# A decoder trunk's feed-forward stages: sums of weight quarters by adding transfers and on VectorE instead of GpSimd

## The chip, the cores and the metric

The kernel runs on one core of a Trainium2 chip. The metric is the device time of one execution in microseconds, as the median of several runs. TensorE does the matrix products (its 128x128 weight loads are shown apart from the matmuls); VectorE, ScalarE (ACT) and GpSimd (POOL) work beside it; SyncE (SP) issues the transfers from HBM. Each engine works off its own queue of instructions in order, and waits at an instruction until the semaphores that it names have been reached.

## The reference

A trunk of two layers on x of 512 tokens by 1024, all in float32. Each layer is a half-step feed-forward, a mixer (layer 0: gated linear recurrence and mLSTM heads; layer 1: sparse attention), and a second half-step feed-forward; then a last RMSNorm. The change touches the four feed-forwards alone:

```python
def rmsnorm(x, g):
    xf = x.astype(jnp.float32)
    y = xf * lax.rsqrt(jnp.mean(xf * xf, axis=-1, keepdims=True) + EPS)
    return (y * g.astype(jnp.float32)).astype(x.dtype)

def swiglu_ffn(x, w_gu, w_down):        # D_MODEL = 1024, D_FF = 2816
    gate, up = jnp.split(x @ w_gu, 2, axis=-1)
    return (jax.nn.silu(gate) * up) @ w_down
```

A layer adds half of `swiglu_ffn(rmsnorm(x, g), ...)` to x.

## The kernel before

Everything lies with the features on the 128 partitions and the 512 tokens along the free axis. A float32 operand is held as two fp32r halves: `hi`, a copy by ACT, and `lo`, the rest, by one subtraction. A product is three matmuls (hi hi, hi lo, lo hi; `mm3`, L172 to L176). Stages run in the order f0a (first feed-forward of layer 0), ab (mixer), f0b, f1a, nsa (mixer), f1b.

A feed-forward (`ffn`, L369 on) has 22 blocks of 128 hidden units. The first four (`CLASSIC`) are done plainly, gate and up each with weights of 128x1024 loaded and split by `wload` (L162 to L170; for the blocks 2 and 3 GpSimd makes `lo`). Meanwhile `Quarters` (L238 to L276) makes sums of quarters of the normalized x (K halves by token halves), splits each (ACT L255, VectorE L256), and two of the sums are GpSimd's (L263, L270). The other 18 blocks are "pairs": gate and up of a block as one 2x2 product by seven multiplications instead of eight (Winograd's form), each of 12 matmuls of 128x256, so 84 for a pair.

`Pair.load` (L291 to L317) brings a pair's weights as four quarters of 128x512: three loads on SP (512, 256 and 256 KB), four sums by GpSimd (L301 to L304), and four splits, each an ACT copy (L310) and a VectorE subtraction (L311), three of 128x1024 and one of 128x512. The raw quarters and sums lie in two buffers `ra` and `rc` (named r in the trace); there are two such sets, taken in turn, so that the loads of a pair wait until the splits of the pair two before have read theirs. The split halves lie in five buffers, taken in turn: three pairs `whi`, `wlo`, and two `wx`.

The products `p1` to `p7` (L323 to L363) come in the order p1, p7, p3 of the pair before, p6, p2, p4, p5; the last pair of a stretch ends p5, p4, p3. They share accumulators: bank `a` takes the first, sixth, fifth and third products one after another, `e` the seventh and fourth, and a bank of its own the second. After each the sum so far is read out: by ACT (L327, L340, L345, L360) or added by VectorE (L333, L350, L355). L362 multiplies the two halves into the hidden block, and ACT L380 and VectorE L381 split that.

After 8, 16 and 22 hidden blocks the down projection adds what is there into X (L444 to L451): eight tiles of `wd`, each loaded, split (L168, L169) and multiplied. So each feed-forward has three stretches of pairs, of 4, 8 and 6, with a down projection (D) behind each. The code orders TensorE's instructions by hand (`manual_schedule`); the other engines' order comes from a scheduler by priorities (`SAHEAD` for a pair's load and splits, `EV` for what empties a bank), so it is seen in the built program alone. In stage ends GpSimd also adds the squares for the next norm (L115), whose root (L141), row sums and broadcast R (L142 to L149) the next stage needs.

## Time and profile before

| | us |
|---|---|
| median of 3 runs (2118.14 to 2119.45) | 2118.43 |
| the profiled execution | 2126.54 |
| its span, first to last instruction | 2124.8 |
| TensorE busy | 2019.0 (95%) |
| VectorE busy | 1432.3 (67%) |
| ACT busy | 1015.2 (48%) |
| GpSimd busy | 858.3 (40%) |
| mean granted clock of TensorE | 0.974 of full |

The shares are means over all stages: where TensorE is idle, and for whom it waits there, is read from the waits and from the windows of the single stretches.

### The profile page before, as it was taken

To read this page: it belongs to the slowest core of one execution; us is meant where nothing else is said; L and a number is where in the kernel's file an instruction comes from. 1 tells how busy PE (TensorE), PEld (TensorE's weight loads), DVE (VectorE), ACT (ScalarE), POOL (GpSimd) and SP (SyncE) were. 2 spreads that over 40 slices of the span, in tenths; PEclk is the share of its full clock that TensorE was granted. 3 is DMA by queue.
4 is the path that set the end of the run, shared out by engine and by line. 5 is a ranking of instruction groups with operands and counts; after the bars stand their busy time and mean duration, and the time that the engine had idled before them with its cause. 6 is when DMAs were issued, how large, how long until landed. Compare 5 with 4: busy or idle time off the path is not lost.

```text
span 2124.8 us, 30587 instructions
## 1 busy us (share of the span) xinstructions
PE 2019.0 (95%) x11896; PEld 1753.4 (83%) x11896; DVE 1432.3 (67%) x2021; ACT 1015.2 (48%) x1828; POOL 858.3 (40%) x602
## 2 busy tenths in 40 slices
PE   7999999989998999999999999999999989999997
PEld 5889889767787889898798989877777667889896
DVE  4957757488658759485866947443877778659474
ACT  4535436445544435254543525434877754435252
POOL 6425523243134427163433614202655554427152
PEclk8999999999899999999999999999999999999998
DMA  4233322222132323233232333321100032323212
GB/s 160 80 110 95 115 75 75 90 80 90 60 99 80 108 81 112 83 101 94 80 110 90 100 94 95 119 84 60 36 16 30 17 114 70 100 90 108 86 61 84
DMA packets 73585, 182.09 MB, mean 86 GB/s; under 512 B 7264, under 2 KB 8032, under 8 KB 73440
## 3 DMA queue, kind: packets, MB, share of 16 engines
q1 hardware_dynamic: 73296, 180.06, 26.7%
q8 instruction: 93, 1.52, 0.3%
q14 instruction: 52, 0.43, 0.1%
q10 hardware_dynamic: 144, 0.09, 0.0%
HBM read 178.02 MB, written 2.10 MB: 85 GB/s over the span
## 4 chain that ended last, share of the span: by engine, by line
PE 75%; DVE 12%; issue 4%; ACT 3%; POOL 3%; DMA 1%; SPq 0%; POOLq 0%; DVEq 0%; ACTq 0%
PE ps L174 18%; PE ps L175 18%; PE ps L176 18%; PE pt L175 3%; PE pt L176 3%; PE pt L174 3%; PE px L977 2%; PE pt L772 2%; DVE wx L311 1%; DVE wlo L169 1%; DMA r<-wgu 1%; PE pt L993 1%; DVE h L381 1%; DVE t L362 1%; DVE wlo L311 1%
## 5 line engine op out<-in xcount | busy, mean ns | idle before, releaser
L301 POOL TENSOR_TENSOR r<-r,r 128x512 f32<-128x512 f32 x72 | 124.0, 1723 | 627.7 <-DMA r<-wgu 587.8
L168 ACT ACTIVATE whi<-raw 128x1024 fp32r<-128x1024 f32 (+2 forms) x196 | 193.2, 987 | 368.9 <-PE ps L175 268.2
L175 PE MATMUL ps<-h,whi 128*128 128x512 f32 x704 | 277.2, 394 | 0.5 <-DVE h L381 0.5
L174 PE MATMUL ps<-h,whi 128*128 128x512 f32 x704 | 276.3, 393 | 0.9 <-ACT h L380 0.9
L176 PE MATMUL ps<-h,wlo 128*128 128x512 f32 x704 | 276.5, 393 | 0.0
L311 DVE TENSOR_TENSOR wlo<-r,whi 128x1024 fp32r<-128x1024 f32 (+1 forms) x174 | 237.2, 1365 | 50.3 <-ACT whi L310 48.9
L310 ACT ACTIVATE whi<-r 128x1024 fp32r<-128x1024 f32 (+1 forms) x174 | 165.5, 951 | 188.5 <-PE ps L175 129.4
L169 DVE TENSOR_TENSOR wlo<-raw,whi 128x1024 fp32r<-128x1024 f32 (+2 forms) x150 | 186.7, 1246 | 76.4 <-ACT whi L168 71.6
L450 DVE SCALAR_TENSOR_TENSOR X<-ps,X 128x512 f32<-128x512 f32 x96 | 66.4, 691 | 253.9 <-PE ps L176 253.9
L169 POOL TENSOR_TENSOR wlo<-raw,whi 128x1024 fp32r<-128x1024 f32 (+1 forms) x46 | 108.7, 2364 | 257.0 <-ACT whi L168 247.5
L311 DVE TENSOR_TENSOR wx<-r,wx 128x1024 fp32r<-128x1024 f32 (+1 forms) x114 | 170.2, 1493 | 57.5 <-ACT wx L310 57.1
L174 PE MATMUL ps<-x,whi 128*128 128x512 f32 x432 | 179.7, 416 | 0.4 <-ACT x L103 0.4
L174 PE MATMUL ps<-qB,whi 128*128 128x256 f32 x520 | 148.5, 286 | 25.0 <-DVE t L355 25.0
L176 PE MATMUL ps<-x,wlo 128*128 128x512 f32 x432 | 171.5, 397 | 0.0
L175 PE MATMUL ps<-x,whi 128*128 128x512 f32 x432 | 171.0, 396 | 0.3 <-DVE x L104 0.3
L175 PEld LDWEIGHTS ps<-h,whi 128*128 128x128 f32 x704 | 132.9, 189 | 31.0 <-DVE h L381 2.3
L174 PEld LDWEIGHTS ps<-h,whi 128*128 128x128 f32 x704 | 133.0, 189 | 30.7 <-ACT h L380 1.8
L176 PEld LDWEIGHTS ps<-h,wlo 128*128 128x128 f32 x704 | 132.8, 189 | 28.6
L115 POOL TENSOR_TENSOR acc<-acc,t 128x512 f32<-128x512 f32 x48 | 74.8, 1558 | 189.4 <-ACT t L113 178.3
L175 PE MATMUL ps<-qB,whi 128*128 128x256 f32 x520 | 146.4, 282 | 0.0
L176 PE MATMUL ps<-qB,wlo 128*128 128x256 f32 x520 | 146.4, 282 | 0.0
L303 POOL TENSOR_TENSOR r<-r,r 128x512 f32<-128x512 f32 x72 | 134.3, 1865 | 5.3
(341 smaller groups left out, 5897.7 us busy)
## 6 DMA issues: line engine op xcount, KB each, us to landing
r<-wgu SPq DMA_DIRECT2D x72, 512.0 KB, 3.9
r<-wgu SPq DMA_DIRECT2D x144, 256.0 KB, 2.8
raw<-wd SPq DMA_DIRECT2D x64, 512.0 KB, 3.5
raw<-wgu SPq DMA_DIRECT2D x30, 512.0 KB, 3.6
raw<-wd SPq DMA_DIRECT2D x32, 384.0 KB, 3.1
raw<-ab_fm SPq DMA_DIRECT2D x21, 512.0 KB, 3.5
raw<-nsa_fm SPq DMA_DIRECT2D x17, 512.0 KB, 3.5
raw<-ab_out SPq DMA_DIRECT2D x8, 512.0 KB, 3.6
```

Source lines behind the costliest of these rows:

```text
L115: nc.gpsimd.tensor_add(acc, acc, sq)
L168: nc.scalar.activation(hi[:, :n], raw[:, :n], AF.Copy)
L169: (eng or nc.vector).tensor_sub(lo[:, :n], raw[:, :n], hi[:, :n].bitcast(F32))
L174: nc.tensor.matmul(ps, wh, xh, start=start, stop=False, skip_group_check=on)
L175: nc.tensor.matmul(ps, wh, xl, start=False, stop=False, skip_group_check=on)
L176: nc.tensor.matmul(ps, wl, xh, start=False, stop=stop, skip_group_check=on)
L301: nc.gpsimd.tensor_sub(ra[:, 1], rc[:, 3], ra[:, 0])
L303: nc.gpsimd.tensor_sub(ra[:, 2], rc[:, 1], ra[:, 0])
L310: nc.scalar.activation(hi[:, :m], src, AF.Copy)
L311: nc.vector.tensor_sub(lo[:, :m], src, hi[:, :m].bitcast(F32))
L450: nc.vector.scalar_tensor_tensor(X[i], ps, 0.5, X[i], op0=OP.mult, op1=OP.add)
L772: nc.tensor.matmul(p2[m][:, :155].rearrange("p (g n) -> p g n", g=5), w[:, q * 256 + m * P:q * 256 + (m + 1) * P], tt[:, :, n:n + 8 * 30 + ...
```

## The change

In each pair, the four GpSimd sums go. The quarters are now loaded so that two of the four positions of `ra` hold the one quarter and two the other (a source with a repeated part), and a third transfer, issued by GpSimd, adds another quarter to the two middle positions while it lands (`accum_op`). Two sums remain and are VectorE's (L309, L310). The sums differ in sign from before, so that the quarters of x whose names begin with B are negated. In the classic part, VectorE makes the low halves and quarter sums that were GpSimd's. The first product is copied by ACT from bank `a` to a second bank `b`, on which the second product then accumulates, so that VectorE's add L333 goes. The fifth product is copied out by ACT to a buffer `u4`, from which VectorE adds (L362). Lines behind L261 are 1 to 8 further down.

```diff
@@ -252,26 +252,31 @@
             def split(self, name, src):
                 t = blk(self.qb[QS.index(name)], F32R, f"q{name}")
                 hi, lo = (t[:, n * 4 * H:(n + 1) * 4 * H].rearrange("p (k t) -> p k t", k=4) for n in range(2))
-                nc.scalar.activation(hi, src, AF.Copy)
-                nc.vector.tensor_sub(lo, src, hi.bitcast(F32))
+                if name[0] == "B":
+                    nc.scalar.activation(hi, src, AF.Copy, scale=-1.0)
+                    nc.vector.scalar_tensor_tensor(lo, src, -1.0, hi.bitcast(F32), op0=OP.mult, op1=OP.subtract)
+                else:
+                    nc.scalar.activation(hi, src, AF.Copy)
+                    nc.vector.tensor_sub(lo, src, hi.bitcast(F32))
                 self.Q[name] = hi, lo
             def before(self):
                 b11, b12, b21, b22 = self.f
                 nc.vector.tensor_sub(b22, b12, b22)
                 self.split("B11", b11)
-                nc.gpsimd.tensor_sub(b12, b12, b11)
+                nc.vector.tensor_sub(b12, b12, b11)
                 self.split("Q7", b22)
                 nc.vector.tensor_sub(b11, b11, b22)
                 self.split("Q6", b11)
             def after(self):
                 q6, q5, b21, b22 = self.f
-                nc.gpsimd.tensor_add(b22, q5, q6)
                 self.split("B21", b21)
                 nc.vector.tensor_sub(b21, b21, q6)
                 self.split("Q4", b21)
                 self.split("Q5", q5)
+                nc.vector.tensor_add(b22, q5, q6)
                 self.split("B22", b22)
         turns = [0, 0]
@@ -295,15 +300,16 @@
                     ra, rc = (blk(rb[2 * (turns[1] % 2) + i], F32, f"r{i}")[:, :4 * T]
                               .rearrange("p (s c) -> p s c", s=4) for i in range(2))
                     turns[1] += 1
-                    nc.sync.dma_start(ra[:, 0:4:3], w[0].rearrange("p (s c) -> p s c", s=2))
-                    nc.sync.dma_start(rc[:, 3], w[1][:, :T])
-                    nc.sync.dma_start(rc[:, 0], w[1][:, T:])
-                    nc.gpsimd.tensor_sub(ra[:, 1], rc[:, 3], ra[:, 0])
-                    nc.gpsimd.tensor_add(rc[:, 1], rc[:, 0], rc[:, 3])
-                    nc.gpsimd.tensor_sub(ra[:, 2], rc[:, 1], ra[:, 0])
-                    nc.gpsimd.tensor_sub(rc[:, 2], ra[:, 3], ra[:, 2])
-                    for src, names in ((ra[:, 0:2], ("B11", "Q7")), (ra[:, 2:4], ("Q6", "B21")),
-                                       (rc[:, 0:2], ("Q4", "Q5")), (rc[:, 2:3], ("B22",))):
+                    both = lambda src: src.unsqueeze(1).to_broadcast([P, 2, T])
+                    nc.sync.dma_start(ra[:, 0:2], both(w[0][:, :T]))
+                    nc.sync.dma_start(ra[:, 2:4], both(w[1][:, T:]))
+                    nc.sync.dma_start(rc[:, 0], w[0][:, T:])
+                    nc.gpsimd.dma_start(ra[:, 1:3], both(w[1][:, :T]), accum_op=OP.add)
+                    nc.vector.tensor_add(rc[:, 1], ra[:, 0], ra[:, 2])
+                    nc.vector.tensor_add(rc[:, 2], rc[:, 0], rc[:, 1])
+                    for src, names in ((ra[:, 0:2], ("B11", "Q7")), (rc[:, 0:2], ("B21", "Q6")),
+                                       (ra[:, 2:4], ("Q5", "Q4")), (rc[:, 2:3], ("B22",))):
                         hi, lo = parts()
                         m = len(names) * T
                         src = src.rearrange("p s c -> p (s c)")
@@ -321,17 +327,16 @@
                     mm3(ps[:, :H], wh[:, ks], wl[:, ks], xh[:, k], xl[:, k], start and k == 0, k == 3, not start)
             def p1(self):
-                self.a, self.t1 = psum(), tp.tile([P, T], F32, name="t1", bufs=3)
+                self.a, self.b, self.t1 = psum(), psum(), tp.tile([P, T], F32, name="t1", bufs=3)
                 self.product(self.a, "B11", True)
                 with tc.high_priority(offset=EV):
-                    nc.scalar.activation(self.t1[:, :H], self.a[:, :H], AF.Copy)
+                    nc.scalar.activation(self.b[:, :H], self.a[:, :H], AF.Copy)
             def p2(self):
-                b = psum()
-                self.product(b, "B21", True)
+                self.product(self.b, "B21", False)
                 with tc.high_priority(offset=EV):
-                    nc.vector.tensor_add(self.t1[:, :H], b[:, :H], self.t1[:, :H])
-                nc.scalar.activation(self.t1[:, :H], self.t1[:, :H], AF.Silu)
+                    nc.scalar.activation(self.t1[:, :H], self.b[:, :H], AF.Silu, scale=-1.0)
             def p7(self):
                 self.e, self.t2 = psum2(), tp.tile([P, T], F32, name="t2", bufs=3)
@@ -351,13 +356,15 @@
             def p5(self):
                 self.product(self.a, "Q5", False)
+                u4 = tp.tile([P, H], F32, name="u4", bufs=1)
                 with tc.high_priority(offset=EV):
-                    nc.vector.tensor_add(self.t2[:, H:], self.a[:, :H], self.t2[:, H:])
+                    nc.scalar.activation(u4, self.a[:, :H], AF.Copy)
+                    nc.vector.tensor_add(self.t2[:, H:], u4, self.t2[:, H:])
             def p3(self):
                 self.product(self.a, "B22", False)
                 with tc.high_priority(offset=EV):
-                    nc.scalar.activation(self.t1[:, H:], self.a[:, :H], AF.Silu)
+                    nc.scalar.activation(self.t1[:, H:], self.a[:, :H], AF.Silu, scale=-1.0)
                 with tc.high_priority(offset=EV // 2):
                     nc.vector.tensor_mul(self.t2, self.t1, self.t2)
                     self.down(self.t2)
@@ -394,9 +401,7 @@
             at = (19, 27) if first else (13, 18)
             wait = []
             for j in range(CLASSIC):
-                eng = nc.gpsimd if j > 1 else None
-                (gh, gl), (uh, ul) = first if first and j == 0 else (wload(wgu[j, 0], eng=eng),
-                                                                     wload(wgu[j, 1], eng=eng))
+                (gh, gl), (uh, ul) = first if first and j == 0 else (wload(wgu[j, 0]), wload(wgu[j, 1]))
                 pg, pu = psum(), psum2()
                 seq = [(k, w) for k in range(KT) for w in range(2)]
                 if j:
```

What the scheduler makes of it, on VectorE's queue. The numbers behind `r` and `t` tell buffers of different pairs apart. First place, the second stretch of f0a, about one pair's time; `L311` before is the split that is `L317` now. Before:

```order
L311 TENSOR_TENSOR wx_1644<-r_1632,wx_1644 128x1024 [waits DVE_49,DMAHW4_49,PE_49,Activation_49]
L362 TENSOR_TENSOR t_1424<-t_1409,t_1424 128x512 [waits DVE_49,Activation_49]
L311 TENSOR_TENSOR wx_1641<-r_1632,wx_1641 128x1024 [waits PE_49,Activation_49]
L381 TENSOR_TENSOR h_326<-t_1424,h_326 128x512 [waits Activation_49]
L333 TENSOR_TENSOR t_1533<-ps,t_1533 128x256 [waits PE_49]
L311 TENSOR_TENSOR wlo<-r_1633,whi 128x1024 [waits DMAHW6_49,Activation_49]
L350 TENSOR_TENSOR t_1548<-pt,t_1548 128x256 [waits PE_49]
L355 TENSOR_TENSOR t_1548<-ps,t_1548 128x256 [waits PE_49]
L311 TENSOR_TENSOR wlo<-r_1633,whi 128x512 [waits Activation_49]
```

And now; r_1632 is the `ra` and r_1633 the `rc` of one pair, r_1755 the `ra` of the next, and DMASW the semaphore of the adding transfer:

```order
L317 TENSOR_TENSOR wlo<-r_1509,whi 128x512 [waits PE_49,Activation_49]
L362 TENSOR_TENSOR t_1424<-u_1505,t_1424 128x256 [waits Activation_49]
L317 TENSOR_TENSOR wx_1643<-r_1633,wx_1643 128x1024 [waits PE_49,Activation_49]
L369 TENSOR_TENSOR t_1424<-t_1409,t_1424 128x512 [waits DVE_49,Activation_49]
L317 TENSOR_TENSOR wx_1640<-r_1632,wx_1640 128x1024 [waits PE_49,Activation_49]
L388 TENSOR_TENSOR h_326<-t_1424,h_326 128x512 [waits Activation_49]
L309 TENSOR_TENSOR r_1756<-r_1755 128x512 [waits DMAHW7_49,DMAHW0_49,DMASW0_49]
L317 TENSOR_TENSOR wlo<-r_1632,whi 128x1024 [waits PE_49,Activation_49]
L355 TENSOR_TENSOR t_1548<-pt,t_1548 128x256 [waits PE_49]
```

The sum L309 of the next pair (r_1756 from r_1755), which waits for that pair's adding transfer, now stands ahead of the last split of this pair's `ra` (`wlo<-r_1632`), which stands ahead of the eviction L355. Before, the next pair's first instruction (the split `wx_1644` from r_1632, which waits for its load) stood behind the last split of the pair ahead of it (`wlo` from r_1509).

Second place, the end of that stretch: the last pair's evictions and the first weights of the down projection (`raw`). Before:

```order
L381 TENSOR_TENSOR h_945<-t_2041,h_945 128x512 [waits Activation_49]
L333 TENSOR_TENSOR t_2150<-ps,t_2150 128x256 [waits PE_49]
L169 TENSOR_TENSOR wlo<-raw,whi 128x1024 [waits Activation_49]
L355 TENSOR_TENSOR t_2165<-ps,t_2165 128x256 [waits PE_49]
L350 TENSOR_TENSOR t_2165<-pt,t_2165 128x256 [waits PE_49]
L169 TENSOR_TENSOR wlo<-raw,whi 128x1024 [waits Activation_49]
L362 TENSOR_TENSOR t_2165<-t_2150,t_2165 128x512 [waits DVE_49,Activation_49]
L169 TENSOR_TENSOR wlo<-raw,whi 128x1024 [waits DMAHW2_49,PE_49,Activation_49]
```

And now:

```order
L369 TENSOR_TENSOR t_2041<-t_2026,t_2041 128x512 [waits DVE_49,Activation_49]
L317 TENSOR_TENSOR wx_2532<-r_2524,wx_2532 128x1024 [waits PE_49,Activation_49]
L388 TENSOR_TENSOR h_945<-t_2041,h_945 128x512 [waits Activation_49]
L309 TENSOR_TENSOR r_2632<-r_2631 128x512 [waits DMAHW7_49,DMAHW6_49,DMASW5_49]
L169 TENSOR_TENSOR wlo<-raw,whi 128x1024 [waits PE_49,Activation_49]
L362 TENSOR_TENSOR t_2165<-u_2233,t_2165 128x256 [waits Activation_49]
L310 TENSOR_TENSOR r_2632<-r_2632 128x512 [waits DMAHW0_49,DVE_49]
L355 TENSOR_TENSOR t_2165<-pt,t_2165 128x256 [waits PE_49]
L169 TENSOR_TENSOR wlo<-raw,whi 128x1024 [waits Activation_49]
```

A sum L309 of the second pair of the stretch to come (r_2632 from r_2631) stands ahead of the first split of `raw` and of the last pair's L362 and L355.

Third place, VectorE at the start of f0a, ahead of L142 (the mean squares from which R is made), as a piece of the difference:

```order
-L311 TENSOR_TENSOR wx_555<-r_546,wx_555 128x1024 [waits DMAHW1_49,Activation_49]
 L169 TENSOR_TENSOR wlo<-raw,whi 128x1024 [waits DMAHW0_49,PE_49,Activation_49]
-L311 TENSOR_TENSOR wx_543<-r_523,wx_543 128x512 [waits Activation_49]
-L142 TENSOR_SCALAR ms<-ps 128x4 [waits Activation_49]
+L309 TENSOR_TENSOR r_546<-r_545 128x512 [waits DMAHW3_49,DMAHW1_49,DMASW0_49]
+L317 TENSOR_TENSOR wx_553<-r_545,wx_553 128x1024 [waits Activation_49]
+L309 TENSOR_TENSOR r_523<-r_522 128x512 [waits DMAHW4_49,DMAHW2_49,DMASW1_49]
+L310 TENSOR_TENSOR r_546<-r_546 128x512 [waits DMAHW5_49,DVE_49]
+L310 TENSOR_TENSOR r_523<-r_523 128x512 [waits DMAHW6_49,DVE_49]
+L169 TENSOR_TENSOR wlo<-raw,whi 128x1024 [waits PE_49,DMAHW7_49,Activation_49,Pool_49]
+L317 TENSOR_TENSOR wx_542<-r_523,wx_542 128x512 [waits Activation_49]
+L169 TENSOR_TENSOR wlo<-raw,whi 128x1024 [waits DMAHW0_49,PE_49,Activation_49]
+L142 TENSOR_SCALAR ms<-ps 128x4
```

The first two pairs' sums and two of the classic blocks' splits now stand ahead of L142, where two splits of those pairs stood.

## Rows read from the trace of the kernel before

**Rows 1.** The page, its span and section 1: busy us, share of the span, instructions.

```profile
span 2124.8 us, 30587 instructions
...
PE 2019.0 (95%) x11896; PEld 1753.4 (83%) x11896; DVE 1432.3 (67%) x2021; ACT 1015.2 (48%) x1828; POOL 858.3 (40%) x602
```

**Rows 2.** Waits of PE: who waited <- for whom: us in all, times, longest.

```profile
PE ps L174 <- DVE t L355: 33.1, 22, 3.9
PE pt L175 <- DVE qQ L256: 11.6, 4, 4.7
...
PE ps L174 <- ACT t L327: 6.6, 4, 2.8
```

**Rows 3.** Windows: stretch, length, PE busy (x), granted clock, DMA share, GB/s; twelve stretches of pairs.

```profile
71.50:119.40 47.90, 41.82 (x337) 0.96 0.34 110
...
675.40:727.60 52.20, 43.01 (x337) 0.93 0.29 93
...
1044.00:1092.50 48.50, 42.79 (x337) 0.93 0.33 108
...
1790.20:1840.70 50.50, 42.67 (x337) 0.93 0.26 84
...
sum 781.20, PE 728.95; mean PE 60.75
```

**Rows 4.** Groups by shape, eight-pair stretch of f0b, 772 to 852 us: busy, mean ns.

```profile
L311 DVE TENSOR_TENSOR wlo<-r,whi 128x1024 fp32r<-128x1024 f32 x12 | 17.8, 1487 | 4.8 <-ACT whi L310 4.5
...
L311 DVE TENSOR_TENSOR wx<-r,wx 128x1024 fp32r<-128x1024 f32 x9 | 14.8, 1645 | 4.3 <-ACT wx L310 4.2
...
L362 DVE TENSOR_TENSOR t<-t,t 128x512 f32<-128x512 f32 x7 | 9.2, 1310 | 0.0
...
L355 DVE TENSOR_TENSOR t<-ps,t 128x256 f32<-128x256 f32 x8 | 3.3, 412 | 0.2 <-PE ps L176 0.2
...
L327 ACT ACTIVATE t<-ps 128x256 f32<-128x256 f32 x8 | 3.0, 380 | 4.2 <-PE ps L176 4.2
```

**Rows 5.** Windows, all engines: two stretches of f0b.

```profile
644.00:675.00 31.00, 31.00 (x140) 25.52 (x139) 29.09 (x28) 13.19 (x16) 15.32 (x6) 1.00 0.27 85
771.60:852.90 81.30, 79.47 (x673) 78.67 (x672) 69.25 (x69) 46.61 (x78) 54.48 (x31) 1.00 0.32 104
```

**Rows 6.** Groups by shape, VectorE, down projection of f0b, 853.5 to 896 us.

```profile
L169 DVE TENSOR_TENSOR wlo<-raw,whi 128x1024 fp32r<-128x1024 f32 x5 | 6.1, 1226 | 1.0 <-ACT whi L168 1.0
...
L362 DVE TENSOR_TENSOR t<-t,t 128x512 f32<-128x512 f32 x1 | 0.7, 678 | 0.0
```

**Rows 7.** Groups of GpSimd over the run: busy, mean ns, idle before, releaser.

```profile
L301 POOL TENSOR_TENSOR r<-r,r 128x512 f32<-128x512 f32 x72 | 124.0, 1723 | 627.7 <-DMA r<-wgu 587.8 <-DVE wlo L311 16.6 <-DVE wlo L169 8.1
L169 POOL TENSOR_TENSOR wlo<-raw,whi 128x1024 fp32r<-128x1024 f32 (+1 forms) x46 | 108.7, 2364 | 257.0 <-ACT whi L168 247.5 <-PE pt L149 9.5
```

**Rows 8.** DMA queues, and issues: KB each, median us from issue to landing.

```profile
q1 hardware_dynamic: 73296, 180.06, 26.7%
...
r<-wgu SPq DMA_DIRECT2D x72, 512.0 KB, 3.9
r<-wgu SPq DMA_DIRECT2D x144, 256.0 KB, 2.8
...
raw<-wgu SPq DMA_DIRECT2D x30, 512.0 KB, 3.6
```

**Rows 9.** Timeline, start of f0a: start us, us, what, [idle before <- releaser].

```profile
20.00 1.32 SPq L300 DMA_DIRECT2D r<-wgu  x2
...
36.19 1.26 POOL L304 TENSOR_TENSOR r<-r 128x512 f32<-128x512 f32 x1
...
37.48 0.63 ACT L310 ACTIVATE wx<-r 128x512 fp32r<-128x512 f32 x1 [7.76 <-POOL r L304]
...
40.22 0.15 DVE L142 TENSOR_SCALAR ms<-ps 128x4 f32<-128x4 f32 x1
...
42.97 1.43 PE L149 MATMUL pt<-ident,Rcol 128*128 128x128 f32 x5 [9.07 <-DVE Rcol L130]
```

## The prediction

> **What bounds the kernel.** I read the engines' shares first. TensorE is busy in 2019.0 of 2124.8 us [rows 1], so the most that a change off TensorE can give is about 106 us. The waits of TensorE tell where these lie. The largest, 33.1 us in 22 waits, is a product of a pair that waits for VectorE's L355 [rows 2]: the third product reuses the bank `a`, and L355, which reads the fifth product out of it, stands in VectorE's queue behind weight splits. A second, 11.6 us in four waits (2.9 in each feed-forward), is the wait for the first quarters of x (L256); a third, of 6.6 us, is for ACT's copy of the first product (L327).
>
> Next come the twelve stretches in which TensorE does pairs (the Strassen stretches: 4, 8 and 6 pairs in each of four feed-forwards). They last 781.2 us and TensorE is busy in 729.0 [rows 3], so 52.2 us are idle there. The four first stretches have 6.1, 9.2, 5.7 and 7.8 of this, 28.8 together, and a granted clock of 0.93 to 0.96, which costs length times what is missing: 1.9+3.7+3.4+3.5 = 12.5 us, or 0.43 us for each idle one. So the pair stretches lose about 16.2 us in each feed-forward ((52.2+12.5)/4); this is what the change can win, and its cover.
>
> Why VectorE is late is seen in the forms of its instructions. In the eight-pair stretch of f0b a 128x1024 split takes 1.49 to 1.65 us and a 128x512 multiply (L362) 1.31 [rows 4], with GpSimd busy in 54.5 of 81.3 us [rows 5]. In the next stretch, where GpSimd is almost idle, the same shapes take 1.22 and 0.68 [rows 6]. The instruction that reads a product from PSUM takes 412 ns [rows 4]. The Trainium skill, "SBUF — State Buffer", "Who interferes with whom", says that a VectorE instruction with two SBUF inputs contends with a GpSimd instruction that reads SBUF; the two stretches agree.
>
> **The change, part by part.** *GpSimd's sums go.* Each pair loses four GpSimd sums (the first, L301, takes 1.72 us [rows 7]). VectorE's work in a pair is now 69.25/81.3 of a pair of 9.8 us (7 products of 1.40), so 8.3 us. Without contention its three 128x1024 splits lose about 0.3 us each, L362 and L381, which has the same shape, 0.6 each, and L333 (a 0.41 us add) is dropped; it gains two 128x512 sums at the clean 0.68. That is 8.3−0.9−1.2−0.4+1.4 = 7.2 us, 1.1 less than now. The wait of the third product also loses its cause: ACT copies the bank out (an ACT copy of this shape takes 380 ns [rows 4]), and the third product stands two products behind the fifth, 2.8 us. I take the 33.1 us as gone, with a bound of half of them, since ACT's queue has splits too.
>
> *The classic blocks and quarter sums move to VectorE.* In a feed-forward 4 low splits (2.36 us each over GpSimd's two forms [rows 7]) and 2 quarter sums become 6 VectorE instructions of 1.22, 7.3 us. VectorE is busy in 29.09 of 31 us there, with GpSimd busy in 15.3 [rows 5]. What contention costs follows from the split: 1645−1224 = 0.42 us more, with GpSimd beside it 54.5/81.3 of 1.645 us = 1.1, so 0.38 us for each us of overlap; 15.3×0.38 = 5.8. Paid and won are nearly the same, and I take zero. Bounds: 2 us gained, or 3 lost in front of the quarters (then four waits grow by 3, −12 in all).
>
> *The adding transfer is new*, and the trace has none. A pair's loads were one of 512 KB (3.9 us) and two of 256 KB (2.8) [rows 8]; now they are two of 512 KB, an accumulating one of 512 KB that can start only when both have landed, and one of 256 KB. A plain load of 512 KB takes 3.6 us, and 180.06 MB were 26.7% of the queue's span, which is 567 us or 1.65 us for 512 KB [rows 8]. So a second load adds about 1.6, and both have landed 5.2 us after the issue. For the accumulate the lower bound is a plain one, 3.6. The upper bound is two in a row, 7.2. Nearest to it is a load that reads twice the bytes, 3.6+1.6 = 5.2, which I take. Call the sum of loads and accumulate C: 10.4 us, between 8.8 and 12.4. (The Trainium skill, "DMA: Bandwidth & Descriptors", "Latency and other measured facts", has a first byte at about 1 us for transfers from GpSimd's queue against 0.6 from SP's. No run so far shows it; by it C would be 10.8 and the gain of the sum below would shrink by 34x0.4 = 14 us, an estimate: that is the rival of no change.)
>
> *C matters because of the order.* VectorE's sum L309 of the next pair waits for the accumulate, and in most pairs it stands ahead of the split that frees `ra` of this pair (the first place of the order above). The ring has two pairs, so: last split of pair k, loads and accumulate of k+2 (C), L309 (0.68), last split of k+1 (1.22). The period is C+1.9 = 12.3 us against TensorE's 9.8, and every such pair loses 2.5. A cushion stands against this: the third split can come as early as its pair's start, and is needed five products later, 7.0 us. In an eight-pair stretch five pairs are crossed so: 5×2.5−7 = 5.5, and 0.7 at the end, where L309 stands ahead of the first `wd` split (second place): 6.2. In the six-pair stretch 3.5 on average: 8.7−7 = 1.7. In the first stretch, loaded long before, 0.7, for L309 between two early splits. The wait for the quarters stays, 2.9. That is 11.5 idle, and 0.43×3.6 = 1.5 of clock for the first stretch: 13.0 in each feed-forward, against 16.2. The gain is 4×3.2 = 12.8. When C grows by one microsecond, each feed-forward loses 5+3.5 = 8.5, so the kernel 34.
>
> *The start of f0a.* There TensorE waits 9.07 us for the row R, since ACT's L310 had waited 7.76 us for GpSimd's last sum (L304, which ends at 37.45) and holds VectorE's L142 to 40.22 [rows 9]. After the change VectorE's queue there has two L309 that wait for accumulates (third place). The last plain load of these pairs was issued by 21.3 [rows 9]; the second accumulate lands at about 21.3+3.9+5.2+1.6 = 32.0, and six instructions follow (4×0.68+2×1.22 = 5.2): 37.2, a gain of 3.0. With an accumulate of 7.2 it is 1.0.
>
> **Sum.** 12.8+3.0 = 16 us, and half of the contention outside (the `wd` splits beside GpSimd, at the ends of D stretches) gives perhaps 2 more: 18. The profiled execution takes 2126.5, and would take 2108.5; the median of the runs is 8.1 lower, so 2118.4−18 = **2100**.
>
> **Rivals.** *Slower: the accumulate is late and VectorE stands in line.* From C = 10.9 to 11.0 (an accumulate of 5.8 us) the gain is gone. At the upper bound, C = 12.4, the 18 turn into 18−2.0×34 = −50: 2168. For it: VectorE's queue is in order, and the traffic grows from 1 to 1.25 MB a pair with 0.5 MB more read back. Against it: the DMA engines are busy in only 0.32 of the eight-pair stretch [rows 5].
>
> *The accumulate is as fast as a plain load*, C = 8.8: the period is 10.7, five crossed pairs lose 4.5 and the cushion takes all. Idle is then 0.7+0.7+2.9 and 1.5 of clock, 5.8 in each feed-forward: a gain of 42, with the 5 beside it 47: 2071.
>
> *The change doesn't do what it says*: the third product's wait comes back, on ACT. ACT's queue has the pair's own splits, which wait for the accumulate too, ahead of L361. If half of the 33.1 us stays, the time is 2117, the same as now.
>
> **Chances.** The forecast (C 9.8 to 10.9, some gain) 0.37, its own range 2084 to 2114; fast accumulate 0.20; no change, by the third rival or by C near 10.9, 0.11; slower 0.32. A measurement can tell 0.2%, 4.2 us, from nothing. Most of the forecast and all of the fast case lie beyond it: faster 0.55, within it 0.12, slower 0.33. The range takes the fast case down to a gain of 56, with 2 us of classic work gained, and of the slow case all but the top and the classic loss: 2062 to 2160.
>
> **What would show it.** Right: splits of 1.22 us in the pair stretches, no wait of TensorE for the fifth product, an issue-to-landing of the accumulate near 5.2 us, and VectorE's wait at L309 for the transfer below about 2.5 us a pair. Wrong: a landing near 7, with TensorE's largest wait then on L317's third split and on ACT's L316 in eight-pair stretches; or an idle TensorE at the starts of D stretches behind `wd` splits; or quarters that come later than now. Splits that stay at 1.5 us would say that transfers issued by GpSimd contend as its sums did.

## The result: slower by 6%, and the profile after

The changed kernel takes 2251.28 us (median of 4 runs, 2245.24 to 2259.77) against 2118.28 us before in the same comparison: a ratio of 1.063, with an interval of 1.059 to 1.068. The prediction was 2100, with 2160 as its upper end. The profiled execution has a span of 2243.5 us, 118.7 more than before (the medians differ by 133.0). The page's first lines, which answer to [rows 1]:

```profile
span 2243.5 us, 30712 instructions
...
PE 2049.9 (91%) x11896; PEld 1777.5 (79%) x11896; DVE 1301.1 (58%) x2117; ACT 1028.9 (46%) x1900; POOL 364.9 (16%) x362
```

VectorE has 131 us less to do and GpSimd 493 less, and TensorE still waits more. Its largest waits (who waits <- for whom, us, times, longest), beside [rows 2]:

```profile
PE pt L174 <- ACT t L345: 46.3, 10, 6.9
PE ps L174 <- ACT t L350: 25.4, 9, 5.3
PE ps L174 <- ACT u L361: 23.1, 9, 11.4
PE ps L174 <- ACT h L387: 19.2, 6, 5.1
PE ps L176 <- DVE wlo L169: 13.0, 6, 6.4
```

The wait for L355 is gone, and so is most of the one for the quarters (5.2 us now). In their place TensorE waits for ACT's evictions (reading a sum out of its bank) of the seventh, sixth and fifth products, for the last hidden block (L387), and for the first split of `wd` (L169). None of these instructions takes long; the engine queues behind them tell what holds them. VectorE's own largest wait for a transfer, and one wait by which it reaches ACT's queue (a split of the sum L309), are:

```profile
DVE r L309 <- DMA r<-wgu: 322.3, 61, 9.7
...
ACT wx L316 <- DVE r L309: 53.1, 13, 7.7
```

The stretches of pairs, as in [rows 3] (first and second stretch of f0a, the eight-pair stretch of f0b, the sum over twelve):

```profile
69.10:120.00 50.90, 42.91 (x338) 0.93 0.57 148
170.80:267.60 96.80, 85.29 (x674) 0.93 0.53 134
...
806.30:908.50 102.20, 82.91 (x673) 0.92 0.57 142
...
sum 865.60, PE 753.88; mean PE 62.82
```

The sum was 781.2, so 84.4 us of the 118.7 are lost here, most in the eight-pair stretches. Of the 84.4, idle time has 59.5 (111.7 instead of 52.2). The other 24.9 are TensorE's busy time, which rises from 729.0 to 753.9 for the same matmuls: the granted clock of the eight-pair stretches is 0.92 to 0.93, where it was 0.99 to 1.00 ([rows 5]; the one of f0a before is this):

```profile
164.50:248.40 83.90, 79.82 (x672) 0.99 0.32 101
```

The down projections lose 39.5 us more, and the other stages together are 5.2 shorter. The first two down projections of f0a and the sum over twelve, and then that sum before:

```profile
120.00:170.70 50.70, 47.27 (x194) 0.93 0.33 101
267.60:319.80 52.20, 45.82 (x194) 0.93 0.39 111
...
sum 528.40, PE 499.81; mean PE 41.65
```

```profile
sum 488.90, PE 487.50; mean PE 40.63
```

VectorE is quick, as it was forecast: in the eight-pair stretch of f0b, by shape, beside [rows 4]:

```profile
L317 DVE TENSOR_TENSOR wlo<-r,whi 128x1024 fp32r<-128x1024 f32 x12 | 14.5, 1220 | 2.4 <-ACT whi L316 2.4
L317 DVE TENSOR_TENSOR wx<-r,wx 128x1024 fp32r<-128x1024 f32 x9 | 11.0, 1221 | 2.5 <-ACT wx L316 2.5
L309 DVE TENSOR_TENSOR r<-r 128x512 f32<-128x512 f32 x8 | 5.5, 691 | 39.6 <-DMA r<-wgu 39.6
...
L369 DVE TENSOR_TENSOR t<-t,t 128x512 f32<-128x512 f32 x7 | 4.8, 685 | 0.0
```

The splits take 1.22 us instead of 1.49 to 1.65 and the multiply 0.69 instead of 1.31, so GpSimd's transfers do not slow VectorE as its sums did. Its idle time stands at one line: the eight sums L309 waited 39.6 of these 102 us for transfers. One turn of the loop in the second stretch of f0a, SP's first load and then what follows on all engines (start, duration, what):

```profile
179.80 0.37 SPq L305 DMA_DIRECT2D r<-wgu  x1
```

```profile
187.31 1.19 POOL L308 DMA_DIRECT2D r<-wgu  x1 [17.22 <-DMA r<-wgu]
...
192.80 0.69 DVE L309 TENSOR_TENSOR r<-r 128x512 f32<-128x512 f32 x1 [6.35 <-DMA r<-wgu]
...
193.41 1.22 DVE L317 TENSOR_TENSOR wlo<-r,whi 128x1024 fp32r<-128x1024 f32 x1
...
194.66 0.37 SPq L305 DMA_DIRECT2D r<-wgu  x1
```

SP issued the loads at 179.80; GpSimd issues the adding transfer at 187.31, 7.5 us later; VectorE's L309 starts at 192.80, 5.5 later; the split behind it in the queue frees `ra`, and SP issues the next loads at 194.66, 1.9 later. The turn takes 14.9 us, and TensorE's pair 9.8 before. This turn has slow loads. Counted over the timeline, from the third pair on in the second and third stretches, L309 waits for its transfer 35 times; the medians there are 6.8 us from the first load to the adding transfer, 5.7 from there to L309, and 13.1 from the first load to L309, which is the prediction's C (some turns have a much later L309, so the medians do not add up). The issues with their landing times, beside [rows 8]:

```profile
r<-wgu SPq DMA_DIRECT2D x144, 512.0 KB, 5.5
r<-wgu POOLq DMA_DIRECT2D x72, 512.0 KB, 5.6
raw<-wd SPq DMA_DIRECT2D x64, 512.0 KB, 3.5
r<-wgu SPq DMA_DIRECT2D x72, 256.0 KB, 5.1
```

### The profile page after: what moved, and what is told of

The parts are those of the page before. It is cut to its first block, busy times and chain, and to the rows that moved or that the text cites. A ratio compares the mean times of both kernels' runs of the same rounds, so it can differ in the third digit from the quotient of the medians.

```text
span 2243.5 us, 30712 instructions
## 1 busy us (share of the span) xinstructions
PE 2049.9 (91%) x11896; PEld 1777.5 (79%) x11896; DVE 1301.1 (58%) x2117; ACT 1028.9 (46%) x1900; POOL 364.9 (16%) x362
## 4 chain that ended last, share of the span: by engine, by line
PE 58%; DMA 20%; DVE 11%; issue 6%; ACT 4%; POOL 1%; SPq 0%; POOLq 0%; DVEq 0%; ACTq 0%
DMA r<-wgu 20%; PE ps L174 13%; PE ps L175 13%; PE ps L176 13%; PE pt L174 2%; PE pt L175 2%; PE pt L176 2%; DVE wlo L317 2%; PE px L982 2%; PE pt L777 2%; DVE wx L317 1%; DVE wlo L169 1%; PE pt L998 1%; PE ps L942 1%; PE pt L999 1%
## 5 line engine op out<-in xcount | busy, mean ns | idle before, releaser
L174 PE MATMUL ps<-h,whi 128*128 128x512 f32 x704 | 281.2, 400 | 19.3 <-ACT h L387 19.2
L308 POOL DMA_DIRECT2D r<-wgu x72 | 86.6, 1205 | 1292.6 <-DMA r<-wgu 769.7
L175 PE MATMUL ps<-h,whi 128*128 128x512 f32 x704 | 282.3, 401 | 2.9 <-DVE h L388 2.9
L309 DVE TENSOR_TENSOR r<-r 128x512 f32<-128x512 f32 x72 | 50.7, 704 | 339.4 <-DMA r<-wgu 322.3
L169 DVE TENSOR_TENSOR wlo<-raw,whi 128x1024 fp32r<-128x1024 f32 (+2 forms) x166 | 193.3, 1169 | 71.5 <-ACT whi L168 66.3
L317 DVE TENSOR_TENSOR wlo<-r,whi 128x1024 fp32r<-128x1024 f32 (+1 forms) x174 | 187.7, 1089 | 33.7 <-ACT whi L316 33.7
L174 PEld LDWEIGHTS ps<-h,whi 128*128 128x128 f32 x704 | 135.4, 192 | 52.2 <-ACT h L387 22.3
L175 PEld LDWEIGHTS ps<-h,whi 128*128 128x128 f32 x704 | 135.5, 192 | 34.7 <-DVE h L388 6.2
L316 ACT ACTIVATE wx<-r 128x1024 fp32r<-128x1024 f32 (+1 forms) x114 | 107.8, 945 | 82.4 <-DVE r L309 53.1
L317 DVE TENSOR_TENSOR wx<-r,wx 128x1024 fp32r<-128x1024 f32 (+1 forms) x114 | 124.1, 1089 | 20.8 <-ACT wx L316 17.6
L174 PE MATMUL ps<-qQ,whi 128*128 128x256 f32 x352 | 103.9, 295 | 25.4 <-ACT t L350 25.4
```

The source lines that it names most:

```text
L169: (eng or nc.vector).tensor_sub(lo[:, :n], raw[:, :n], hi[:, :n].bitcast(F32))
L174: nc.tensor.matmul(ps, wh, xh, start=start, stop=False, skip_group_check=on)
L175: nc.tensor.matmul(ps, wh, xl, start=False, stop=False, skip_group_check=on)
L308: nc.gpsimd.dma_start(ra[:, 1:3], both(w[1][:, :T]), accum_op=OP.add)
L309: nc.vector.tensor_add(rc[:, 1], ra[:, 0], ra[:, 2])
L316: nc.scalar.activation(hi[:, :m], src, AF.Copy)
```

## The experiments

All times are medians; the ratio is to the kernel before on the same chip, with its 95% interval.

**e1: four plain loads, all sums on VectorE.**

```diff
-nc.sync.dma_start(ra[:, 0:2], both(w[0][:, :T]))
-nc.sync.dma_start(ra[:, 2:4], both(w[1][:, T:]))
-nc.sync.dma_start(rc[:, 0], w[0][:, T:])
-nc.gpsimd.dma_start(ra[:, 1:3], both(w[1][:, :T]), accum_op=OP.add)
+nc.sync.dma_start(ra[:, 0], w[0][:, :T])
+nc.sync.dma_start(rc[:, 3], w[1][:, :T])
+nc.sync.dma_start(ra[:, 3], w[1][:, T:])
+nc.sync.dma_start(rc[:, 0], w[0][:, T:])
+nc.vector.tensor_add(ra[:, 1], ra[:, 0], rc[:, 3])
+nc.vector.tensor_add(ra[:, 2], ra[:, 3], rc[:, 3])
```

> The changed kernel without the adding transfer: four plain loads of 256 KB in each pair, and all four sums on VectorE (128x512 each). Theory A (the loop of loads, adding transfer and VectorE's in-order sum, 13.0 us of transfers and 1.9 of VectorE for each crossed pair): the loop is short now (loads 6 us), so the eight-pair stretches fall from 95 to 102 us back to about 83 to 88, and the kernel takes 2090 to 2125 us. Theory B (ACT's new copies, from bank to bank and to u4, hold TensorE): they are still there, so the kernel stays above 2200.

Measured: 2099.4 us, ratio 0.991 (0.988 to 0.994). Without the adding transfer, and with loads of 256 KB, the rest of the change is a gain of 1%. ACT's copies are not what costs 133 us, so theory B falls. TensorE still waits for u4 there, 18.6 us in twelve times:

```profile
PE ps L174 <- ACT u L361: 18.6, 12, 3.7
```

**e2: one ordering edge on VectorE.** The first sum of a pair may not stand ahead of the split of `ra[:, 2:4]` of the pair before (an edge of order alone, no wait):

```diff
-nc.vector.tensor_add(rc[:, 1], ra[:, 0], ra[:, 2])
+t = nc.vector.tensor_add(rc[:, 1], ra[:, 0], ra[:, 2])
+if freed:
+    tc.add_manual_dep(t.ins, freed.pop().ins.name, mybir.DependencyInfo(
+        mybir.DependencyClass.NoSync, mybir.DependencyReason.DATA), reason="order")
...
-nc.vector.tensor_sub(lo[:, :m], src, hi[:, :m].bitcast(F32))
+s = nc.vector.tensor_sub(lo[:, :m], src, hi[:, :m].bitcast(F32))
+if names[0] == "Q5":
+    freed.append(s)
```

> The changed kernel with one ordering edge on VectorE: the first sum of a pair may not stand ahead of the third split of the pair before. Same transfers, same work. Theory A: the loop no longer passes through two pairs in turn (13 us of transfers have two pairs' time, 19.7 us), eight-pair stretches near 84 to 88 us, the kernel 2095 to 2140. Theory C (the transfers themselves are too slow, 1.25 MB and an accumulate in each pair, whatever the order): stays above 2200.

Measured: 2109.47 us, ratio 0.996 (0.993 to 0.998). The same work and the same transfers in another order take 142 us less, more than the whole loss, and theory C falls: the transfers are not too slow as such. VectorE's wait for the adding transfer goes from 322.3 to 141.4 us, and what is left lies beside TensorE's work:

```profile
DVE r L310 <- DMA r<-wgu: 141.4, 50, 8.6
```

**e5 and e6: the edge in two parts.** e5 gives the edge to all pairs but the second of a second or third stretch (whose sum stands ahead of the first `wd` split, the second place of the order above); e6 gives it to those alone (`if before and second`). The lines of e5 against e2:

```diff
-if freed:
+before = freed.pop() if freed else None
+if before and not second:
...
-p = Pair(quarters.Q, downs(j)).load(wgu[j], rb)
+p = Pair(quarters.Q, downs(j)).load(wgu[j], rb, j0 > 0 and j == j0 + 1)
```

> The changed kernel with the ordering edge for all pairs but the second pair of the second and third stretches, whose first sum stays ahead of the down projection's first split of wd and of the last pair's evictions. Theory A in two parts: the pair stretches recover as with the full edge (eight-pair stretches 78 to 89 us), and what the sums at the eight transitions cost stays: down projections of 8 and 8 blocks stay at 49 to 52 us where they were so, about 4 to 6 us at five or six transitions, so 2109 plus 25 to 35: 2130 to 2145. If the transitions cost only the 0.7 us that the prediction gave them: 2109 to 2115.

> The counterpart: the ordering edge for the second pair of the second and third stretches alone; within the stretches the crossed order stays. Theory A: down projections fall back to 44 to 46 us, eight-pair stretches stay at 95 to 102, so 2251 less 25 to 40: 2210 to 2226. If a late sum at a transition was only a consequence of the loop within the stretch: 2240 or more.

Measured: e5 2142.16 us (1.009, 1.006 to 1.012), e6 2213.51 us (1.044, 1.040 to 1.048). So the crossing within the stretches costs 109 us and the transitions 38, together 147 where the full edge gives 142 (by the ratios, each to the kernel before on its own chip, 115 and 41, where the full edge gives 143). Each part has its place. TensorE's windows over the twelve pair stretches of e5 (sum of lengths, TensorE busy), and over its twelve down projections:

```profile
sum 765.80, PE 721.87; mean PE 60.16
```

```profile
sum 528.30, PE 501.35; mean PE 41.78
```

The pair stretches have come back (865.6 to 765.8), the down projections have not (528.4 to 528.3). In e6 it is the other way round:

```profile
sum 862.00, PE 753.08; mean PE 62.76
```

```profile
sum 501.10, PE 491.20; mean PE 40.93
```

How a transition loses is seen in the changed kernel at 272 us, the end of f0a's second stretch:

```profile
272.71 0.69 DVE L309 TENSOR_TENSOR r<-r 128x512 f32<-128x512 f32 x1 [7.11 <-DMA r<-wgu]
273.32 1.22 DVE L169 TENSOR_TENSOR wlo<-raw,whi 128x1024 fp32r<-128x1024 f32 x1
...
274.60 0.79 PE L176 MATMUL ps<-h,wlo 128*128 128x512 f32 x1 [6.38 <-DVE wlo L169]
```

VectorE had stood at L309 for 7.11 us. Behind it are the first split of `wd`, for which TensorE waits 6.38 us, and the last pair's evictions; and when TensorE starts again its next matmul takes 0.79 us where the 704 of its line have a mean of 397 ns: twice as long. From 274.6 to 276.2 us the granted clock is 0.50, the lower of its two levels (1.2 of 2.4 GHz), and over the whole of this down projection 0.93.

**e3: the accumulator copies alone, on the kernel before.** GpSimd's sums stay; p1's copy goes to a second bank, p2 accumulates on it (so that the add L333 goes), p5 is copied to u4.

```diff
-nc.scalar.activation(self.t1[:, :H], self.a[:, :H], AF.Copy)
+nc.scalar.activation(self.b[:, :H], self.a[:, :H], AF.Copy)
...
-self.product(b, "B21", True)
+self.product(self.b, "B21", False)
...
-nc.vector.tensor_add(self.t2[:, H:], self.a[:, :H], self.t2[:, H:])
+nc.scalar.activation(u4, self.a[:, :H], AF.Copy)
+nc.vector.tensor_add(self.t2[:, H:], u4, self.t2[:, H:])
```

> The kernel before with only the other accumulator copies: the first product's copy from bank to bank with the second accumulating on it, and the fifth product copied by ACT to u4. GpSimd's sums stay. Theory A: these copies cost nothing and take away the wait for VectorE's eviction (33 us): 2085 to 2118. Theory B: ACT is late with them, 2130 or more.

Measured: 2108.67 us, ratio 0.995 (0.993 to 0.997). Nearly half of the third product's wait stays, at ACT's copy instead of VectorE's add (33.1 us before):

```profile
PE ps L174 <- ACT u L354: 14.4, 7, 3.4
```

**e8: e1 without u4** (VectorE adds the fifth product from its bank).

> The first experiment (four plain loads, all sums on VectorE) without the copy to u4: VectorE adds the fifth product from its bank, as before. VectorE is busy in some 94% of the eight-pair stretches there. If VectorE's queue is what holds the bank, the old wait comes back, 15 to 35 us in all, and the kernel takes 2110 to 2130; if splits without contention leave VectorE on time, the 18.6 us for which TensorE waits for u4 there go down and it takes 2085 to 2098.

Measured: 2102.06 us, ratio 0.990 (0.989 to 0.992), between the two expectations. TensorE waits for the fifth product 26.4 us in 24 times, now for VectorE's add, and 18.6 in e1 for u4; the two kernels cannot be told apart.

**e4: a plain transfer in place of the adding one** (`accum_op` left out; two of the seven weight sums are then wrong, and with them the two that VectorE makes from them).

> The changed kernel with the adding transfer made a plain one from the same queue, so that two of the seven weight sums are wrong; everything else stays. The packets of the adding transfer take about 0.20 us against 0.105 for plain ones, so the transfer should land about 1.5 us sooner. Theory A: crossed pairs cost 1.5 us less each, 34 us per us, so about 50 us less: 2185 to 2215. If only the place in the queues mattered and not the transfer's length: 2240 or more.

Measured: 2147.75 us, ratio 1.012 (1.010 to 1.015): 103 us less than the change, where some 50 were expected. Its issues:

```profile
r<-wgu POOLq DMA_DIRECT2D x72, 512.0 KB, 4.0
```

The gain is more than 34 us for each microsecond of the loop. Counted as above, C is 13.1 us in the changed kernel and 10.9 here (36 waits), so 103 us go with 2.2, or 47 us for each; in e10 below 72 go with 1.7, or 42. The prediction's 34 is idle time alone; with its own 0.43 us of clock for each idle one it would be 49. How much of the 103 lies at the transitions was not separated. From the same queue the transfer lands in 4.0 us when it is plain and in 5.6 when it adds. The 1.6 us between them is what the prediction took for reading 512 KB more, but it is not shown to be that: the trace also has the plain one in 9,216 packets of 4 KB and the adding one in 18,432 of 2 KB. (The Trainium skill, "Collectives: The Full Stack", "Why ReduceScatter is half of AllGather", says of a collective's reduction that it is slow for its two source reads and not for the add. No run here shows whether that holds for an adding load.)

**e10: each row's 4 KB read once instead of one half twice**, for both 512 KB loads (some weight sums are then wrong).

```diff
-nc.sync.dma_start(ra[:, 0:2], both(w[0][:, :T]))
+nc.sync.dma_start(ra[:, 0:2], w[0].rearrange("p (s c) -> p s c", s=2))
...
```

> The changed kernel with the two 512 KB loads reading each row's 4 KB once, where the change reads one 2 KB half twice; bytes, packets of 2 KB at the destination and queues stay, some of the weight sums are wrong. If the repeated source makes the loads slow, the first lands in 3.9 us as before instead of 5.5, and the kernel takes 2170 to 2200. If the landing is that of two or three loads which share the engines, it stays near 5.5, and so does the time, 2235 to 2260.

Measured: 2179.73 us, ratio 1.028 (1.024 to 1.032). One turn in the same stretch, the first load's issues on SP and the adding transfer's on GpSimd:

```profile
188.73 0.33 SPq L305 DMA_DIRECT2D r<-wgu  x1
...
201.28 0.33 SPq L305 DMA_DIRECT2D r<-wgu  x1
```

```profile
194.16 1.19 POOL L308 DMA_DIRECT2D r<-wgu  x1 [11.59 <-DVE wx L317]
```

The adding transfer is issued 5.4 us after the first load, which is also the median of 37 such waits (6.8 in the changed kernel, 7.5 in its turn above), and the turn takes 12.6 us. So with plain rows both loads have landed nearly when the prediction had it (5.2 us); with the repeated source they have not. The packets do not stay as expected: the trace has these loads in packets of 4 KB, and in 2 KB ones in the changed kernel. The landing of each:

```profile
r<-wgu SPq DMA_DIRECT2D x144, 512.0 KB, 4.3
```

**e12: the repeat made two transfers.** Each load that reads a 2 KB half of each row twice becomes two loads of 256 KB.

```diff
-nc.sync.dma_start(ra[:, 0:2], both(w[0][:, :T]))
-nc.sync.dma_start(ra[:, 2:4], both(w[1][:, T:]))
+for i in range(4):
+    nc.sync.dma_start(ra[:, i], w[0][:, :T] if i < 2 else w[1][:, T:])
```

> The changed kernel with each 512 KB load that reads a 2 KB half of each row twice made two plain loads of 256 KB, one after the other; the same bytes, the adding transfer as it is. If it is the repeat inside one transfer that made the loads take 1.4 us longer than a plain source (tenth experiment), the adding transfer is issued about 5.5 us after the first load as there, the crossed period falls from 14.8 to some 13 us, and the kernel takes 2175 to 2205. If it is the 2 KB packets or the second reading of the same bytes, it stays at 6.9 or more (one issue more), and the kernel at 2240 to 2275.

Measured: 2279.67 us, ratio 1.075 (1.071 to 1.079). The adding transfer is issued 6.8 us after the first load:

```profile
189.93 1.76 SPq L306 DMA_DIRECT2D r<-wgu  x4
```

```profile
196.72 1.20 POOL L308 DMA_DIRECT2D r<-wgu  x1 [14.00 <-DMA r<-wgu]
```

The median over 68 pairs is 6.5 us, and over all 72 of the changed kernel 6.9, so most of the delay against e10 is not the repeat inside one transfer. Whether it is rows read in pieces of 2 KB, the packets of 2 KB, or the second reading of the same rows, is not told apart. Nor is it shown why e12 takes 28 us more than the changed kernel though these loads are no later; VectorE's waits at L309 are 390.1 us in all there, and 322.3 in the changed kernel.

**e7 and e9: the third load behind the adding transfer.** Both have GpSimd issue the 256 KB load, e7 without the `with` line.

```diff
-nc.sync.dma_start(rc[:, 0], w[0][:, T:])
-nc.gpsimd.dma_start(ra[:, 1:3], both(w[1][:, :T]), accum_op=OP.add)
+add = nc.gpsimd.dma_start(ra[:, 1:3], both(w[1][:, :T]), accum_op=OP.add)
+with tc.issue_after(add.ins):
+    nc.gpsimd.dma_start(rc[:, 0], w[0][:, T:])
```

> The changed kernel with the third load (256 KB to rc) issued by GpSimd behind the adding transfer instead of by SP ahead of it. It isolates the load's share of the loop: if the transfers in flight share the engines packet by packet, the two loads that the adding transfer waits for land 1.0 to 1.3 us sooner (5.6 to 5.9 us instead of 6.9 after the first issue), and at 45 us per us the kernel takes 2190 to 2215. If the landing of 5.5 us comes from reading the same rows twice, it stays, and so does the time: 2240 to 2260.

Measured: 2244.23 us, ratio 1.057 (1.053 to 1.061). On GpSimd's queue the scheduler had put it ahead of the adding transfer, so it told nothing about what it was made for.

> The seventh experiment again, now with an ordering edge on GpSimd: the third load (256 KB) stands behind the adding transfer there (in the seventh it stood ahead of it, so it was still in flight with the two loads). If the transfers in flight share the engines, the two loads land about 5.6 to 6.0 us after the first issue instead of 6.9, the loop is 1 us shorter, and the kernel takes 2195 to 2220. If their landing does not depend on the third load, 2235 to 2260.

Measured: 2230.8 us, ratio 1.050 (1.044 to 1.055), between the two expectations. One turn, SP's first load and GpSimd's adding transfer:

```profile
190.21 0.37 SPq L305 DMA_DIRECT2D r<-wgu  x1
```

```profile
197.23 1.18 POOL L307 DMA_DIRECT2D r<-wgu  x1 [12.41 <-DMA r<-wgu]
```

The loads take 7.0 us until the adding transfer is issued. The median over 34 such waits is 6.8, the same as in the changed kernel, so the third load does not hold the two others; C falls by 0.4, from 13.1 to 12.7, behind them. The third load is a small part.

**e11: e9's load with the edge of e2.**

> The ordering edge on VectorE (second experiment) together with the third load behind the adding transfer. With the edge the transfers have 19.7 us for two pairs and 13 are used, so a shorter C should give little: 2095 to 2110 against 2109 of the edge alone, from the starts of stretches. If the third load, now late, holds the second sum, 2115 or more.

Measured: 2132.77 us, ratio 1.005 (1.002 to 1.008): worse than the edge alone. The second sum (L315 here) now waits for transfers too, 14.4 us in 14 times, as the second expectation has it; that this is the whole 23 us is not shown:

```profile
DVE r L311 <- DMA r<-wgu: 137.1, 48, 7.4
...
DVE r L315 <- DMA r<-wgu: 14.4, 14, 3.5
```

**e13: the separate loads of e12 with the edge of e2.**

> The same loads with the ordering edge on VectorE. The edge alone takes 2109. With faster loads 2095 to 2108, from the starts of stretches where TensorE still waits; with loads as slow as before, 2105 to 2115.

Measured: 2089.94 us, ratio 0.984 (0.981 to 0.987), the fastest kernel of all, with the change's adding transfers. The loads of the slowest kernel, e12, are here in the fastest. VectorE's wait falls further:

```profile
DVE r L310 <- DMA r<-wgu: 105.3, 50, 7.0
```

Why it is 20 us faster than the edge alone was not taken apart: the loads land in pieces, and the scheduler's order moved with them.

## Why the prediction was wrong, point by point

*The wait of the third product*: half right. L355 no longer holds TensorE, but the third product now waits for ACT's copy: 14.4 us in e3, 18.6 in e1, 23.1 in the changed kernel. The prediction took the 33.1 us as gone, with half of them as its bound. e3 puts a price on the copies alone: a gain of 0.5%.

*The wait for the quarters* was forecast to stay at 2.9 us in each feed-forward; it fell from 11.6 to 5.2 in all.

*GpSimd's sums slow VectorE*: right. Splits take 1.22 us. e1, with the sums on VectorE, has the gain of everything but the transfers: 1%.

*The loop of loads, adding transfer, L309 and split*: the mechanism was right, at the place named. e2 shows that the crossed order is the whole loss, and e5 and e6 that the loop within the stretches has about three quarters of it. Two sizes were wrong.

The first is C. The accumulate was forecast at 5.2 us and took 5.7 by the median (5.5 in the turn above); VectorE's 1.9 was 1.9. The loads were forecast at 5.2 from issue until the adding transfer can start, and took 6.8 (7.5 in the turn above). About 1.4 of these 1.6 go when the loads read plain 4 KB rows (e10). The step that failed is "a second load adds about 1.6, and both have landed 5.2 us after the issue". C was 13.1, above the upper bound of 12.4, for which only the accumulate had been given a bound, and the loads none. With C = 13.0 (the turn above) the prediction's own sum gives 34x2.6 = 88 us more, 2188.

The second is what a microsecond of C costs: "each feed-forward loses 5+3.5 = 8.5, so the kernel 34". e4 and e10 have 47 and 42. The step had no clock in it: the prediction charges 0.43 us for each idle one in the first stretches, and nothing for the idle time of the crossed pairs. At C = 13.0 its terms have 135 us idle in the pair stretches and 6 of clock, 141 in all and 76 more than before. Measured are 112 idle and 24.9 more busy time, 84.4 more than before. That these totals are close is luck: too much idle time stands against a clock that was left out.

*The transitions*: mis-sized, and the largest part of what 2188 leaves open. The prediction gave them 0.7 us at the end of an eight-pair stretch, because it counted L309's place but not that the loop had by then no cushion left. The down projections lost 39.5 us, and e6 puts the transitions at 38 us in all.

*What is won when the loop does not bind*: mis-sized. The fast rival was 2071, of which 42 us were to be won in the pair stretches. With the edge alone, where the loop does not bind the stretches, the kernel takes 2109. The pair stretches and the down projections of e2 sum up to:

```profile
sum 765.40, PE 725.43; mean PE 60.45
```

```profile
sum 498.70, PE 490.92; mean PE 40.91
```

The pair stretches win 15.8 us there and the down projections lose 9.8. TensorE still waits for the sixth product's copy, u4 and R:

```profile
PE ps L174 <- ACT t L356: 17.1, 6, 5.2
PE ps L174 <- ACT u L367: 9.6, 5, 3.2
PE pt L149 <- DVE Rcol L130: 8.8, 2, 7.6
```

e13, with the same edge, takes 2090, so 2109 is not the least that the mended order allows.

*The start of f0a*: a gain of 3.0 was forecast. R's first matmul (L149) starts at 42.31 instead of 42.97 [rows 9], so 0.7 came, because VectorE could start the second L309 at 36.74 and not at 32.0, by its timeline.

*The chances*: the slower rival was the right one, at 0.32, with its place and its point of decision (an accumulate of 5.8 us, or C near 11), but even its upper case was 2168. It was put below the forecast with C's least certain half taken to be the accumulate; the loads missed by more. (By the Trainium skill, "DMA: Bandwidth & Descriptors", "Latency and other measured facts", the first byte of a transfer from GpSimd's queue comes at about 1 us, against 0.6 from SP's. In e4 the plain one from there lands in 4.0 us, and SP's `raw` in 3.5; they read other rows beside other transfers, so no run isolates the difference.)

## What to carry to other kernels

When a transfer's end releases an instruction, look at what stands behind that instruction in its engine's queue, and whether one of these frees the buffer that the next such transfer needs: then the chain has one pair's time and not two. Here an ordering edge was worth 142 us, more than either faster part (103 and 72). A bound belongs on every term of such a chain, the ordinary loads too: those of 512 KB that read half rows twice landed in 5.5 us, where loads of the same size took 3.9 before. A price for idle time belongs on all of it: the clock that the prediction charged in one stretch was lost in the others too. Moving work off a contended engine and moving its inputs onto a longer chain are two changes; make them apart, since here the first gives 1% and the second took 7.

## What the runs showed of the hardware that was not expected

A transfer that adds to SBUF 512 KB lands in 5.4 to 5.9 us, by the median of each run, and a plain one from the same queue in its place in 4.0 (e4; that one is in packets of 4 KB and the adding one in 2 KB, so the 1.6 us are not shown to be the add's alone). It does not slow VectorE's splits (1.22 us). GpSimd's issue of it takes 1.2 us, SP's of a load 0.4. A load of 512 KB that reads a 2 KB half of each row twice lands in 5.5 us, one that reads the 4 KB row once in 4.3, with the same bytes and the same number of loads in flight. Such a source is not slow in every place: e4's plain transfer also reads a half twice, from GpSimd's queue when those loads have landed, and lands in 4.0. And idle time of TensorE costs more than itself: in stretches with waits of 5 to 7 us the granted clock was 0.92 to 0.93, and busy time over the twelve pair stretches grew by 24.9 us for the same matmuls.
